# Down stages: activation sums on VectorE among the gate/up pairs, first output chunks through ScalarE and adding transfers

## The chip, the cores and the metric

One core of one Trainium2 chip runs the whole kernel as one launch. The time is the device time of that launch in microseconds (us). Below, PE is TensorE, DVE is VectorE, ACT is ScalarE, POOL is GpSimd and SP is SyncE; SP issues most plain transfers, and POOL issues all adding ones (transfers that add what they bring to what stands in the tile).

## The reference, cut to what matters

Two layers act on h, 512 tokens of width 1024, all in float32. The hidden width of a SwiGLU is 2816.

```python
h += 0.5 * swiglu(rmsnorm(h), w_gate, w_up, w_down)      # FFN1
h += W_out @ mixer(rmsnorm(h))     # layer 0: banded + dilated attention; layer 1: 2-D neighbourhood attention
h += 0.5 * swiglu(rmsnorm(h), w_gate, w_up, w_down)      # FFN2
h += sigmoid(rmsnorm(h) @ W_gate) * (p[i] @ W_ple)       # gate with a per-layer input

def swiglu(x, w_gate, w_up, w_down):
    return (jax.nn.silu(x @ w_gate) * (x @ w_up)) @ w_down
```

The change touches the four products with `w_down` (2816 x 1024), what stands just ahead of them (the gate and up products), and the norm that follows each.

## The kernel before, in words

**Precision.** Every float32 product is three matmuls of a reduced type: an operand x is split into hi, a copy made by ACT (L148), and lo = x - hi, made mostly by DVE (L149); then hi·hi + lo·hi + hi·lo is summed in PSUM.

**Gate and up.** The hidden width is cut into 22 chunks of 128, and `ffn` (L401 on) makes each by one "pair" (gate and up together). Pairs 0 to 3 (`pair_front`) use the chunks `xg` of h that are not yet divided by the root mean square, and multiply by it afterwards; pair 4 (`pair`) and pairs 5 to 21 (`pair_fast`, seven half-size products in place of eight, L371 to L373) use chunks split again by `halves` between the first pairs. A pair leaves one activation tile a[m], 128 x 512.

**Down.** `down` (L435 on) computes the product with w_down by seven half-size products in place of eight. The 2816 rows are halved into a[0..10] and a[11..21] (K2 = 11 chunks each), the 512 tokens into a left and a right 256, the 1024 columns into two halves. Four weight quarters b11, b12, b21, b22 are brought in six units of up to two chunks. A unit's product is 12 matmuls of 128 x 512 (L463 to L465), one whole product 66. The seven products run in three phases:

- phase 1, per unit: r1 from x1 (a[k] after its right half lost that of a[11+k], L432) and b11; r2 from x2 (a[11+k]) and b21; r3 from x1 and b11+b12;
- phase 2: rb from x3 and b12+b22; r1 goes on with b11 added, rc with b21 added too. x3 and the left half of a[11+k] are sums of activations, made in place by POOL (L510, L511, L513);
- phase 3: r3 goes on with b22 and x4 (the left half of a[11+k]).

Weights of a unit come by SP into one of five `wr` tiles (`load`), the sums of quarters are made in place by adding transfers that POOL issues (`add`, L454), and `parts` splits the tile anew after each. So POOL's queue holds both the sums of activations and the adding transfers, in the order in which a scheduler placed them at build time.

**The tail of a down stage.** After phase 3 the results stand with tokens on the partitions. For each of the eight chunks m of h, PE transposes four blocks into one of two `tr` banks (L545), and DVE adds half of them to the residual (L549), which SP had loaded from DRAM into `hs` (L538). `norm_split` then makes the next norm's hi (ACT, L211) and lo (DVE, L212), `norm_square` the square (ACT, L217) and its sum over chunks (L224, on POOL for most). POOL stores the chunk back (L562, L580). Chunks 0 to 3 take their halves from r1/r2 and rc, chunks 4 to 7 from c22 (ready after phase 2) and c2 (ready after phase 3). After FFN1 the mixer's projections read these splits; after FFN2 `ple` does: its first gate matmuls (L173 to L175) run chunk by chunk as the splits come.

## Time and profile before

| what | value |
|---|---|
| time, median of 3 (lowest, highest) | 2138.43 us (2136.97, 2143.73) |
| the profiled execution: its own time, its span | 2138.97 us, 2137.2 us |
| PE busy | 2032.2 us (95%) |
| DVE busy | 1620.7 us (76%) |
| ACT busy | 1131.5 us (53%) |
| POOL busy | 526.1 us (25%) |
| mean granted PE clock | 0.981 |

A row of a group reads: line, engine, operation, tile written <- tiles read, shapes, count | busy us, mean ns of one | idle time of the engine ahead of them, and what ended it. A row of windows reads: from:to in us, length, then busy us (and count) of PE, PEld, DVE, ACT and POOL, the granted PE clock, the share of time for which the 16 DMA engines were busy, and GB/s. A row of the chain of waits reads: start, length, who. A row of transfers reads: tile <- source, queue, count, KB each, median us from issue to landing. The four down stages are the windows that begin at 238.7, 900.3, 1327.7 and 1922.9 us.

### The profile page before, as it was taken

How to read it: one execution, taken by the hardware profiler on the slowest of the kernel's cores; microseconds unless marked ns; L12 is line 12 of the kernel's file. 1: busy time of each engine (PE TensorE's matmuls, PEld its weight loads, DVE VectorE, ACT ScalarE, POOL GpSimd, SP SyncE). 2: the span in 40 equal slices, each digit the busy share in tenths (PEclk: the TensorE clock that was granted, in tenths of full speed). 3: DMA queues.
4: the chain of work that ended last, by engine and by line, in shares of the span. 5: the costliest groups of instructions: out<-in, count | busy, mean ns of one | idle time of the engine just before them, and what ended most of it. 6: DMA issues, size and time to landing. Idle time of an engine off the chain costs nothing.

```text
span 2137.2 us, 33010 instructions
## 1 busy us (share of the span) xinstructions
PE 2032.2 (95%) x12294; PEld 1785.7 (84%) x12294; DVE 1620.7 (76%) x2571; ACT 1131.5 (53%) x1902; POOL 526.1 (25%) x534
## 2 busy tenths in 40 slices
PE   9999979899999999979899999798999999998888
PEld 6999857779788899957688999577888889996766
DVE  8787966688766887876678878767788587888575
ACT  5455645477645455645454556454666445554542
POOL 0011642432212001371320013713000200128231
PEclk9999989999999999999999999999999999999899
DMA  6677589543325576579554775796433446656971
GB/s 199 169 190 184 135 189 264 136 89 90 94 60 172 131 186 183 149 176 195 206 161 125 189 185 149 175 192 209 124 109 95 158 123 183 178 147 164 193 251 40
DMA packets 128049, 339.10 MB, mean 159 GB/s; under 512 B 23824, under 2 KB 31504, under 8 KB 127888
## 3 DMA queue, kind: packets, MB, share of 16 engines
q1 hardware_dynamic: 97728, 241.52, 34.3%
q0 software_dynamic: 30016, 95.44, 25.4%
q8 instruction: 96, 1.57, 0.3%
q14 instruction: 65, 0.53, 0.1%
q10 hardware_dynamic: 144, 0.04, 0.0%
HBM read 308.62 MB, written 17.27 MB: 152 GB/s over the span
## 4 chain that ended last, share of the span: by engine, by line
PE 69%; DVE 10%; DMA 7%; issue 6%; POOL 4%; ACT 3%; SPq 0%; DVEq 0%; POOLq 0%; ACTq 0%
PE mm L373 6%; PE mm L372 6%; PE mm L371 6%; PE mm L174 6%; PE mm L173 6%; PE mm L175 6%; DMA wr<-in_dn_dram 5%; DVE wl L149 3%; PE sc L373 3%; PE sc L372 3%; PE sc L371 3%; PE sc L173 2%; PE sc L175 2%; PE sc L174 2%; DVE act L212 1%
## 5 line engine op out<-in xcount | busy, mean ns | idle before, releaser
L148 ACT ACTIVATE wh<-wr 128x1024 fp32r<-128x1024 f32 (+1 forms) x503 | 516.0, 1029 | 577.7 <-DMA wr<-in_dn_dram 148.5
L149 DVE TENSOR_TENSOR wl<-wr,wh 128x1024 fp32r<-128x1024 f32 (+1 forms) x503 | 632.7, 1262 | 223.0 <-ACT wh L148 219.8
L373 PE MATMUL mm<-act,wl 128*128 128x256 f32 x1088 | 307.9, 283 | 0.0
L372 PE MATMUL mm<-act,wh 128*128 128x256 f32 x1088 | 307.9, 283 | 0.0
L371 PE MATMUL mm<-act,wh 128*128 128x256 f32 x1088 | 307.9, 283 | 0.0
L174 PE MATMUL mm<-act,wh 128*128 128x512 f32 (+1 forms) x648 | 258.2, 399 | 4.4 <-DVE act L212 4.2
L173 PE MATMUL mm<-act,wh 128*128 128x512 f32 (+1 forms) x648 | 256.7, 398 | 3.9 <-DVE act L689 2.5
L175 PE MATMUL mm<-act,wl 128*128 128x512 f32 (+1 forms) x648 | 256.7, 396 | 3.3 <-DVE wl L149 3.3
L371 PEld LDWEIGHTS mm<-act,wh 128*128 128x128 f32 x1088 | 208.9, 192 | 0.2
L372 PEld LDWEIGHTS mm<-act,wh 128*128 128x128 f32 x1088 | 208.9, 192 | 0.2
L373 PEld LDWEIGHTS mm<-act,wl 128*128 128x128 f32 x1088 | 208.9, 192 | 0.0
L349 POOL DMA_DIRECT2D wr<-in_gu_dram x68 | 60.0, 882 | 495.7 <-DVE wl L149 195.0
L371 PE MATMUL sc<-act,wh 128*128 128x256 f32 x544 | 154.0, 283 | 0.0
L372 PE MATMUL sc<-act,wh 128*128 128x256 f32 x544 | 154.0, 283 | 0.0
L373 PE MATMUL sc<-act,wl 128*128 128x256 f32 x544 | 154.0, 283 | 0.0
L149 DVE TENSOR_TENSOR act<-act,act 128x512 fp32r<-128x512 f32 (+1 forms) x192 | 150.7, 817 | 4.2 <-ACT act L148 4.1
L174 PEld LDWEIGHTS mm<-act,wh 128*128 128x128 f32 x648 | 123.9, 191 | 31.8 <-DVE act L212 9.0
L224 POOL TENSOR_TENSOR ssq<-ssq,tmp 128x512 f32<-128x512 f32 x48 | 70.1, 1460 | 324.0 <-ACT tmp L217 323.3
L173 PEld LDWEIGHTS mm<-act,wh 128*128 128x128 f32 x648 | 123.4, 191 | 28.2 <-issue 2.7
L175 PEld LDWEIGHTS mm<-act,wl 128*128 128x128 f32 x648 | 123.8, 191 | 26.6 <-DVE wl L149 4.5
L454 POOL DMA_DIRECT2D wr<-in_dn_dram x96 | 83.8, 901 | 185.1 <-DVE wl L149 122.2
L464 PE MATMUL mm<-wl,act 128*128 128x512 f32 x264 | 104.7, 397 | 14.0 <-DVE wl L149 14.0
(232 smaller groups left out, 4883.2 us busy)
## 6 DMA issues: line engine op xcount, KB each, us to landing
wr<-in_gu_dram SPq DMA_DIRECT2D x176, 512.0 KB, 4.6
wr<-in_dn_dram SPq DMA_DIRECT2D x80, 512.0 KB, 4.5
wr<-in_dn_dram POOLq DMA_DIRECT2D x80, 512.0 KB, 6.9
wr<-in_gu_dram POOLq DMA_DIRECT2D x68, 512.0 KB, 5.5
rb<-in_gu_dram SPq DMA_DIRECT2D x68, 256.0 KB, 2.6
act<-kept SPq DMA_DIRECT2D x56, 256.0 KB, 5.1
wr<-in_qk_ab_dram SPq DMA_DIRECT2D x20, 512.0 KB, 4.1
kept<-act POOLq DMA_DIRECT2D x32, 256.0 KB, 2.4
```

Source lines behind the costliest of these rows:

```text
L148: self.put(self.nc.scalar.activation(hi, src, AF.Copy))
L149: self.put((lo_eng or self.nc.vector).tensor_tensor(lo, src, hi.bitcast(F32), op=ALU.subtract))
L173: mm(out, stat[0], mov[0], start=start, stop=False)
L174: mm(out, stat[0], mov[1], start=False, stop=False)
L175: return mm(out, stat[1], mov[0], start=False, stop=stop)
L224: self.last_sum = eng.tensor_tensor(self.acc, self.acc, sq, op=ALU.add)
L349: nc.gpsimd.dma_start(rs, w[:, :UNIT], accum_op=ALU.add)
L371: mm(out, w[0][:, c], xs[k][0][:, x], start=start and k == 0, stop=False, skip_group_check=True)
L372: mm(out, w[0][:, c], xs[k][1][:, x], start=False, stop=False, skip_group_check=True)
L373: mm(out, w[1][:, c], xs[k][0][:, x], start=False, stop=stop and k == half - 1, skip_group_check=True)
L454: nc.gpsimd.dma_start(raw, b[:, u.start * T:u.stop * T], accum_op=ALU.add)
L464: mm(p, xh, wl, start=False, stop=False, skip_group_check=True)
```

## The change

- The halves that the down product combines are now the even and the odd hidden chunks: A = a[0::2], B = a[1::2]. The host lays out w_down to match.
- POOL does no arithmetic for the down product. `inner_sums` makes the three 256-wide operations of a chunk pair on DVE, for 9 of the 11 pairs right after the odd gate/up pair that completes it, for the other two in `down`; x3's source is a tile of its own (`sums`). The left half of B is updated on DVE.
- Pair 4 is made by `pair_front`, and `pair` is gone. `halves` splits only the left half of a first-half chunk.
- c2's copy and u3 stand ahead of the last rc product.
- Chunks 0 to 3 of h are transposed among the units of phase 3: ACT evicts each with a factor of 0.5 (L543 in the new numbering), and an adding transfer issued by POOL adds the residual from DRAM (L544). SP loads only the residuals of chunks 4 to 7. The transposes of c22 stand behind phase 3's units 4 and 5. All stores of h stand at the end (L572).
- After down stages the squares are summed on DVE. The first v projection of a mixer takes one bank from the other PSUM pool.

```diff
@@ -31,8 +31,9 @@
 WARM = 12
-FRONT = 4
-FAST = range(5, NF)
+FRONT = 5
+READY = 9
+SPLIT = 2
@@ -220,7 +221,7 @@
         else:
-            eng = nc.vector if c == KC - 1 or self.k == 0 else nc.gpsimd
+            eng = nc.vector if c == KC - 1 or self.k in (0, 1, 3, 5, 7) else nc.gpsimd
@@ -301,20 +302,6 @@
             self.mm3(p, (u[0][:, c:c + P], u[1][:, c:c + P]), xs[k], k == 0, k == KC - 1)
-    def pair(self, w, y):
-
...
-        nc.scalar.activation(t, pgu[0], AF.Silu)
-        nc.vector.tensor_tensor(t, pgu[1], t, op=ALU.mult)
-        return t
-
@@ -323,7 +310,12 @@
             nc.vector.scalar_tensor_tensor(x, self.h[k], self.gain[:, self.k, k:k + 1], self.R, op0=ALU.mult, op1=ALU.mult)
-            out.append(self.split_chunk(x, nc.vector))
+            if k < KC // 2:
+                both = self.act(F32R)
+                out.append((both[:, :H], both[:, H:]))
+                self.split(x[:, :H], *out[-1])
+            else:
+                out.append(self.split_chunk(x, nc.vector))
@@ -407,32 +399,31 @@
         kept = io["xT"].rearrange("p c t -> c p t") if first else self.put_away()
-        x1 = [None] * K2
+        x1, sums = [None] * K2, [None] * K2
...
             if m == NF - 1:
-                for k in range(2):
-                    self.lead_part(x1, a, k)
-            if m < FRONT:
-                r = self.pair_front(gu[i, m], m, first, gu[i, m + 1])
-            elif m in FAST:
-                r = self.pair_fast(gu[i, m], y, t)
-            else:
-                r = self.pair(gu[i, m], y)
+                for k in range(SPLIT):
+                    x1[k] = self.split_chunk(a[2 * k], nc.vector)
+            r = self.pair_front(gu[i, m], m, first, gu[i, m + 1]) if m < FRONT else self.pair_fast(gu[i, m], y, t)
             a.append(r)
+            if m % 2 and m // 2 < READY:
+                sums[m // 2] = self.inner_sums(*a[m - 1:])
...
         self.begin_norm(k_next)
-        self.down(dn[i], a, x1, kept)
-
-    def lead_part(self, x1, a, k):
-
-        if x1[k] is None:
-            right = slice(T // 2, T)
-            self.nc.gpsimd.tensor_tensor(a[k][:, right], a[k][:, right], a[K2 + k][:, right], op=ALU.subtract)
-            x1[k] = self.split_chunk(a[k], self.nc.vector)
-
-    def down(self, w, a, x1, kept):
+        self.down(dn[i], a, x1, sums, kept)
+
+    def inner_sums(self, a, b):
+
+        l, r = slice(0, T // 2), slice(T // 2, T)
+        s, tt = self.act(), self.nc.vector.tensor_tensor
+        tt(a[:, r], a[:, r], b[:, r], op=ALU.subtract)
+        tt(s[:, r], a[:, r], a[:, l], op=ALU.subtract)
+        tt(s[:, l], s[:, r], b[:, r], op=ALU.add)
+        return s
+
+    def down(self, w, a, x1, sums, kept):
@@ -440,7 +431,7 @@
         copy, tt, sub = nc.scalar.activation, nc.vector.tensor_tensor, ALU.subtract
-        pool = nc.gpsimd.tensor_tensor
+        A, B = a[0::2], a[1::2]
@@ -480,12 +471,15 @@
                 for k in ks(u):
-                    self.lead_part(x1, a, k)
+                    if sums[k] is None:
+                        sums[k] = self.inner_sums(A[k], B[k])
+                    if x1[k] is None:
+                        x1[k] = self.split_chunk(A[k], nc.vector)
...
                 for k in ks(u):
-                    x2[k] = self.split_chunk(a[K2 + k], nc.vector)
+                    x2[k] = self.split_chunk(B[k], nc.vector)
@@ -507,76 +501,74 @@
             if s < n:
...
                 for k in ks(u):
-                    pool(a[k][:, r], a[k][:, r], a[k][:, l], op=sub)
-                    pool(a[k][:, l], a[k][:, r], a[K2 + k][:, r], op=ALU.add)
-                    x3[k] = self.split_chunk(a[k], nc.vector)
-                    pool(a[K2 + k][:, l], a[K2 + k][:, l], a[k][:, r], op=ALU.add)
+                    x3[k] = self.split_chunk(sums[k], nc.vector)
+                    tt(B[k][:, l], B[k][:, l], sums[k][:, r], op=ALU.add)
                 product(rb, u, self.parts(raws[s]), x3, l, True, True)
...
                 add(raws[s - 1], b21, u)
+            if s == n + 1:
+                c2 = copied(r1)
+                u3 = [self.act(), self.act()]
+                for i in range(2):
+                    tt(u3[i], c2[i], rb[i], op=sub)
             if s > 1:
...
                     x4[k] = t[:, l], t[:, r]
-                    self.split(a[K2 + k][:, l], *x4[k])
-        c2, c21 = copied(r1), [self.act(), self.act()]
-        u3 = [self.act(), self.act()]
+                    self.split(B[k][:, l], *x4[k])
+        c21 = [self.act(), self.act()]
         for i in range(2):
-            tt(u3[i], c2[i], rb[i], op=sub)
             tt(c21[i], rc[i], u3[i], op=ALU.add)
+        for i in range(2):
             tt(c5[i], c5[i], u3[i], op=sub)
-        c22 = c5
-
-        hs = []
-        for m in range(KC):
-            hs.append(self.act())
+        c22, M = c5, KC // 2
+
+        hs = [self.act() for _ in range(KC)]
+        for m in range(M, KC):
             nc.sync.dma_start(hs[m], kept[m])
-        for u in units:
-            raw = load(b22, u)
-            product(r3, u, self.parts(raw), x4, l, False, True)
         def turned(out, x, j):
...
                 nc.tensor.transpose(out[:, i * P:(i + 1) * P], y[:, j * P:(j + 1) * P], self.ident)
-        def done(m, p, c):
-            h = hs[m]
-            nc.vector.scalar_tensor_tensor(h[:, c], p, 0.5, h[:, c], op0=ALU.mult, op1=ALU.add)
-            self.h[m] = h
-            if c.stop == T and c.start == 0:
-                self.norm_split(m)
-            else:
-                self.norm_split(m, c)
-
-        M = KC // 2
-        for m in range(M):
-            p = self.tbank()
+        def first_half(m):
+            p, h = self.tbank(), hs[m]
             turned(p[:, l], c11, m)
             turned(p[:, r], c21, m)
-            done(m, p, slice(0, T))
-            nc.gpsimd.dma_start(self.kept[m], hs[m])
-            self.norm_square(m)
-        for m in range(0, M, 2):
+            nc.scalar.activation(h, p, AF.Copy, scale=0.5)
+            nc.gpsimd.dma_start(h, kept[m], accum_op=ALU.add)
+            self.h[m] = h
+            self.norm_split(m)
+
+        def second_half(m, x, c):
             p = self.tbank()
             for j in range(2):
-                turned(p[:, j * H:(j + 1) * H], c22, m + j)
+                turned(p[:, j * H:(j + 1) * H], x, m - M + j)
             for j in range(2):
-                done(M + m + j, p[:, j * H:(j + 1) * H], r)
+                h = hs[m + j]
+                nc.vector.scalar_tensor_tensor(h[:, c], p[:, j * H:(j + 1) * H], 0.5, h[:, c], op0=ALU.mult, op1=ALU.add)
+                self.h[m + j] = h
+                self.norm_split(m + j, c)
+
+        for i, u in enumerate(units):
+            raw = load(b22, u)
+            product(r3, u, self.parts(raw), x4, l, False, True)
+            if i in (2, 3):
+                first_half(2 * i - 4)
+                first_half(2 * i - 3)
+            elif i > 3:
+                second_half(M + 2 * i - 8, c22, r)
         for c in (l, r):
...
                 tt(c2[i][:, c], r3[i][:, c], c2[i][:, c], op=sub)
-        for m in range(0, M, 2):
-            p = self.tbank()
-            for j in range(2):
-                turned(p[:, j * H:(j + 1) * H], c2, m + j)
-            for j in range(2):
-                done(M + m + j, p[:, j * H:(j + 1) * H], l)
-        for m in range(M, KC):
+        for m in range(M, KC, 2):
+            second_half(m, c2, l)
+        for m in range(KC):
             nc.gpsimd.dma_start(self.kept[m], hs[m])
@@ -655,11 +647,11 @@
         return out
-    def project_v(self, src, view, rcol, parts=True):
-
-
-        nc = self.nc
-        banks = [self.bank(), self.bank()]
+    def project_v(self, src, view, rcol, parts=True, banks=None):
+
+
+        nc = self.nc
+        banks = banks or [self.bank(), self.bank()]
@@ -852,7 +844,8 @@
             if i < 2:
-                f = lambda: v.__setitem__(key, self.project_v(io["v_ab"][i], nat, self.rcol))
+                f = lambda: v.__setitem__(key, self.project_v(io["v_ab"][i], nat, self.rcol, banks=None if i else [
+                    self.sbank(), self.bank()]))
@@ -1169,7 +1162,7 @@
                 fill.append((("v", n // 2), 2, lambda i=n // 2: vs.__setitem__(
-                    i, self.project_v(io["v_c"][i], nat, self.rcol))))
+                    i, self.project_v(io["v_c"][i], nat, self.rcol, banks=None if i else [self.sbank(), self.bank()]))))
@@ -1375,7 +1368,7 @@
 def _quarters(w):
-    return w.reshape(2, K2, P, 2, T).transpose(0, 3, 2, 1, 4).reshape(4, P, K2 * T)
+    return w.reshape(K2, 2, P, 2, T).transpose(1, 3, 2, 0, 4).reshape(4, P, K2 * T)
```

POOL's queue at the first down stage (`act` are activation tiles, `wr` weight tiles; lines 432 to 513 are the sums, 454 the adding transfers). Before:

```order
L510 TENSOR_TENSOR act_283<-act_283 128x256
L511 TENSOR_TENSOR act_283<-act_283,act_1417 128x256
L510 TENSOR_TENSOR act_365<-act_365 128x256
L511 TENSOR_TENSOR act_365<-act_365,act_1541 128x256
L432 TENSOR_TENSOR act_1169<-act_1169,act_2533 128x256
L454 DMA wr_2774<-in_dn_dram 128x1024
L513 TENSOR_TENSOR act_1417<-act_1417,act_283 128x256
```

and now (445 is the line of the adding transfers of weights):

```order
L341 DMA wr_2677<-in_gu_dram 128x1024
L445 DMA wr_2807<-in_dn_dram 128x1024
L445 DMA wr_2852<-in_dn_dram 128x1024
L445 DMA wr_2921<-in_dn_dram 128x1024
L445 DMA wr_2990<-in_dn_dram 128x1024
```

The sums are gone from between the transfers, whose own order is what it was.

ACT's queue at the end of the first down stage (`wh_3937` and the like are the first splits of the mixer's weights, L211 is hi, L217 the square). Before:

```order
L148 ACTIVATE wh_3872<-wr_3871 128x1024
L148 ACTIVATE wh_3937<-wr_3936 128x1024
L148 ACTIVATE wh_3991<-wr_3990 128x1024
L211 ACTIVATE act_3725<-act_3601,gain 128x512
L217 ACTIVATE ssq_3730<-act_3601 128x512
L211 ACTIVATE act_3738<-act_3603,gain 128x512
L217 ACTIVATE tmp_3743<-act_3603 128x512
```

and now (L543 is the eviction, L212 hi, L218 the square):

```order
L543 ACTIVATE act_3611<-tr_3677 128x512
L149 ACTIVATE wh_3882<-wr_3881 128x1024
L212 ACTIVATE act_3684<-act_3611,gain 128x512
L218 ACTIVATE ssq_3826<-act_3611 128x512
L543 ACTIVATE act_3612<-tr_3688 128x512
L149 ACTIVATE wh_3947<-wr_3946 128x1024
L149 ACTIVATE wh_4001<-wr_4000 128x1024
L212 ACTIVATE act_3695<-act_3612,gain 128x512
L218 ACTIVATE tmp_3829<-act_3612 128x512
L543 ACTIVATE act_3613<-tr_3717 128x512
L212 ACTIVATE act_3724<-act_3613,gain 128x512
```

The eviction of a chunk now stands behind hi and square of the chunk before it. On POOL the adding transfer of a chunk and its store stand in turn:

```order
L544 DMA act_3611<-in_xT_dram 128x512
L572 DMA kept_2800<-act_3611 128x512
L544 DMA act_3612<-in_xT_dram 128x512
L572 DMA kept_2800<-act_3612 128x512
L544 DMA act_3613<-in_xT_dram 128x512
```

A store reads the tile that the adding transfer ahead of it writes.

7 lines of the change are left out of this document (removed).

## The prediction, made before the changed kernel ran

> **What bounds the kernel now.** First the page: busy shares and the granted clock.
>
> ```profile
> PE 2032.2 (95%) x12294; PEld 1785.7 (84%) x12294; DVE 1620.7 (76%) x2571; ACT 1131.5 (53%) x1902; POOL 526.1 (25%) x534
> PEclk9999989999999999999999999999999999999899
> ```
>
> PE is busy 95% of the span, so what can be won is idle PE and matmuls at a lower clock, together about 100 us. The windows over the four down stages, and one dense stretch of the same matmuls, show where that lies. Columns: window, length, busy us (count) of PE, PEld, DVE, ACT, POOL, granted clock, DMA share, GB/s.
>
> ```profile
> 238.70:364.70 126.00, 113.26 (x465) 89.27 (x464) 89.11 (x96) 62.17 (x89) 56.17 (x52) 0.95 0.84 203
> 900.30:1027.20 126.90, 111.37 (x464) 88.41 (x463) 89.43 (x96) 62.03 (x89) 56.16 (x52) 0.96 0.83 203
> 1327.70:1454.10 126.40, 113.18 (x464) 89.25 (x463) 88.12 (x94) 61.27 (x89) 56.16 (x52) 0.95 0.83 198
> 1922.90:2050.80 127.90, 113.27 (x464) 89.80 (x463) 89.61 (x96) 62.18 (x89) 56.21 (x52) 0.93 0.83 201
> 984.00:1008.00 24.00, 24.00 (x108) 19.87 (x107) 12.16 (x18) 10.60 (x16) 4.33 (x5) 1.00 0.92 190
> ```
>
> A dense matmul takes about 0.2265 us (24.00 us hold 106 of them, the two at the edges counted as parts). A stage has 7 x 66 = 462: 104.6 us dense. The four take 126.0 + 126.9 + 126.4 + 127.9 = 507.2, so 507.2 - 418.5 = 88.7 us are lost there, 22.2 in each: nearly all that the run loses. The first stage cut by phase (phase 1 ends at 297.6, phase 2 at 349.7):
>
> ```profile
> 238.70:272.00 33.30, 30.67 (x132) 24.08 (x131) 33.30 (x30) 20.98 (x30) 31.26 (x27) 1.00 0.64 155
> 272.00:297.60 25.60, 17.94 (x69) 12.97 (x67) 15.06 (x14) 7.39 (x12) 13.63 (x13) 0.92 0.82 186
> 297.60:309.00 11.40, 8.95 (x22) 6.32 (x23) 5.45 (x7) 5.54 (x8) 3.46 (x4) 0.65 1.03 216
> 309.00:349.70 40.70, 40.70 (x177) 33.56 (x177) 26.31 (x37) 22.31 (x34) 7.82 (x9) 0.98 0.91 197
> 349.70:364.70 15.00, 15.00 (x68) 12.35 (x67) 9.00 (x12) 5.95 (x6) 0.00 (x0) 1.00 0.95 344
> ```
>
> Phases 1 and 2 are 198 matmuls each, 44.85 us dense. Phase 1 takes 58.9 (lost 14.0), phase 2 52.1 (lost 7.3), phase 3 nothing. In the first window DVE is busy all the time and POOL nearly so, with the DMA at 0.64; then the DMA saturates (1.03) and the clock falls to 0.65. The chain of waits through that place:
>
> ```profile
> 283.69 7.64 DMA wr<-in_dn_dram
> 291.90 0.86 POOL wr L454
> 296.63 7.04 DMA wr<-in_dn_dram
> 303.76 1.06 ACT wh L148
> ```
>
> So the stage is late twice: DVE paces phase 1, which delays adding transfers that POOL issues behind its sums, and these then pile up and set the start of phase 2.
>
> **The change part by part. POOL's sums go.** Splits on DVE, in 246 to 272 (POOL adding, two rows) and in 311 to 345 (POOL mostly idle, two rows), then POOL's sums in the whole run:
>
> ```profile
> L149 DVE TENSOR_TENSOR act<-act,act 128x512 fp32r<-128x512 f32 x14 | 16.1, 1184 | 0.0
> L149 DVE TENSOR_TENSOR wl<-wr,wh 128x1024 fp32r<-128x1024 f32 x8 | 13.5, 1688 | 0.0
> L149 DVE TENSOR_TENSOR wl<-wr,wh 128x1024 fp32r<-128x1024 f32 x10 | 12.2, 1223 | 11.0 <-ACT wh L148 11.0
> L149 DVE TENSOR_TENSOR act<-act,act 128x512 fp32r<-128x512 f32 x5 | 3.4, 685 | 0.0
> L432 POOL TENSOR_TENSOR act<-act,act 128x256 f32<-128x256 f32 x44 | 34.1, 775 | 233.9 <-DVE act L398 233.9
> L513 POOL TENSOR_TENSOR act<-act,act 128x256 f32<-128x256 f32 x44 | 60.7, 1389 | 5.6 <-ACT act L148 2.9 <-DVE act L149 2.8
> ```
>
> The same DVE splits take 1184 and 1688 ns while POOL adds, 685 and 1223 without it. With the lower durations, 14 x 0.50 + 8 x 0.465 = 10.7 of DVE's 26 us in that window go: DVE no longer paces phase 1, and the adding transfers issue as soon as their tile is split. What takes DVE's place is the DMA. Its busy time in phases 1 and 2 is share by length: 33.3 x 0.64 + 25.6 x 0.82 + 11.4 x 1.03 + 40.7 x 0.91 = 91.1 us, against 89.7 of dense matmuls. The bytes stay, so even a full DMA leaves 91.1 + 15.0 (phase 3) = 106.1 per stage. At phase 3's share, 0.95, it is 95.9 + 15.0 = 110.9; at 0.91, the share of the flowing part of phase 2, 100.1 + 15.0 = 115.1. I take 0.95, since with DVE free the five `wr` tiles turn round without that pause: 4 x 110.9 = 443.6, a gain of **63.6 us**; bounds 507.2 - 460.4 = 47 and 507.2 - 424.4 = 83.
>
> **The sums among the gate/up pairs.** Front pairs, other pairs, a 256-wide DVE sum, and DVE's wait in each pair:
>
> ```profile
> 30.00:62.00 32.00, 32.00 (x142) 26.20 (x141) 31.85 (x55) 15.96 (x25) 1.96 (x2) 1.00 0.56 112
> 80.00:200.00 120.00, 120.00 (x1002) 120.00 (x1002) 96.51 (x132) 63.89 (x95) 14.89 (x18) 1.00 0.70 181
> L335 DVE TENSOR_TENSOR tmp<-tmp,tmp 128x256 f32<-128x256 f32 x16 | 6.7, 420 | 0.0
> L381 DVE TENSOR_TENSOR act<-mm,act 128x256 f32<-128x256 f32 x68 | 28.9, 424 | 55.2 <-ACT act L380 55.2
> ```
>
> Three sums of 0.42 are 1.26 us per two pairs. In the pairs DVE is busy 96.5 of 120 and stands still 55.2 / 68 = 0.81 us at L381 in each, under a PE that is never idle: hidden. In the front pairs DVE is full (31.85 of 32), and the change gives it a few sums more there; in return pair 4 no longer waits for `halves`. I cost the whole at nothing. Without the cover it is 9 x 1.26 = 11.3 us per FFN at most, 45 in all; that PE is at 32.00 of 32.00 with DVE full already says that the cover holds.
>
> **The tail.** Chunks 0 to 3 leave DVE and SP for ACT and an adding transfer. The rows: eviction, hi, square, sum of squares on POOL and DVE, hi of a half chunk, adding and plain transfers of POOL, and the two kinds of tail from the end of phase 3's third unit on (mixer behind, `ple` behind).
>
> ```profile
> L470 ACT ACTIVATE act<-mm 128x512 f32<-128x512 f32 x16 | 8.5, 584 | 0.0
> L211 ACT ACTIVATE act<-act,gain 128x512 fp32r<-128x512 f32 x48 | 34.0, 716 | 20.9 <-DVE act L1317 10.4 <-DVE act L744 7.8 <-DMA act<-in_xT_dram 2.0
> L217 ACT ACTIVATE tmp<-act 128x512 f32<-128x512 f32 x62 | 37.7, 617 | 10.1 <-DVE act L1300 10.1
> L211 ACT ACTIVATE act<-act,gain 128x256 fp32r<-128x256 f32 x32 | 16.2, 506 | 15.4 <-DVE act L549 15.4
> L224 POOL TENSOR_TENSOR ssq<-ssq,tmp 128x512 f32<-128x512 f32 x48 | 70.1, 1460 | 324.0 <-ACT tmp L217 323.3
> wr<-in_dn_dram POOLq DMA_DIRECT2D x16, 256.0 KB, 5.2
> kept<-act POOLq DMA_DIRECT2D x32, 256.0 KB, 2.4
> 357.90:400.80 42.90, 36.27 (x219) 30.16 (x217) 29.30 (x42) 20.81 (x32) 15.28 (x16) 1.00 0.62 222
> 1020.40:1058.10 37.70, 29.87 (x135) 22.62 (x134) 28.17 (x36) 18.03 (x28) 17.62 (x17) 0.95 0.58 213
> ```
>
> In ACT's new order the eviction of a chunk stands behind hi of the one before, and that hi waits for the adding transfer. So the four chunks go one after another: 0.58 + 5.2 + 0.72 + 0.62 + 0.1 (handing over) = 7.2 us each. A new adding transfer of 256 KB to an h tile has no row; the nearest is the 5.2 of `wr`, below it stands POOL's plain store with 2.4, above it the 7.64 of the chain. Let Z be the end of phase 3's third unit. Eviction 0 ends at Z + 1.7 (four transposes and 0.58), hi 0 at 7.6, hi 3 at 7.6 + 3 x 7.2 = 29.2, its square at 29.8; then four times (2 x 0.506 + 0.617) = 6.5 for chunks 4 to 7: Z + 36.4. Queued behind the waiting ACT are the next weights' splits; on POOL each store waits for the adding transfer ahead of it, and behind it nothing urgent stands but the next chunk's transfer, which is late anyway; SP has four loads of 256 KB fewer, which the adding transfers bring instead; on PE the transposes of chunks 2 and 3 and of c22 wait for the two `tr` banks, so phase 3's last units do too. In `ple`'s tail the eighth chunk's matmuls start at about Z + 37.7 and two more pieces of 2.7 us follow: 43.1 against 37.7, 5.4 slower. In the mixer's tail, PE has other matmuls to fill with: 43.4 against 42.9. PE then idles in pieces of 4 to 5 us. Before, the pause near 290 was followed by 11.4 us at a clock of 0.65, which is 4.0 us of matmul time; I take 2 per tail (bounds 0 and 4). Together 2 x 7.4 + 2 x 2.5 = **20 us lost**, 12 to 28 with the bounds of the clock alone.
>
> The Trainium skill (TensorE: Matmul & The Clock Gate, What's actually happening) halves the clock after about 3.4 us of idle PE; the 0.65 behind a pause of some 4 us agrees, and by it the new pauses of 4 to 5 us would each cost a slow window, which is the upper bound above.
>
> **Small parts.** Sums of squares go from 1460 ns on POOL to DVE, where they lie behind the squares on ACT in either case; c2 ahead of the last product and the bank for v lie beside dense PE: nothing.
>
> **Sum.** 2139.0 - 63.6 + 19.8 = 2095.2 against the profiled execution; the median of the runs shown is 0.5 lower: **2095 us**. Its own range, bounds taken together: 2139 - 83 + 12 = 2068 to 2139 - 47 + 28 = 2120.
>
> **The rivals.**
>
> *The adding transfers land like stores (14 in 100).* If they take 2.4 us, a step is 4.4, hi 3 comes at Z + 4.8 + 13.2 = 18.0, and the tails gain instead of lose: ACT ends at 25.2, `ple`'s tail 6.4 sooner than before, the mixer's by about 3 (its matmuls, less the wait for POOL's sums): 19 in all, so 2139 - 64 - 19 = 2056. For it: 256 KB is small and the DMA is at 0.58 to 0.62 there. Against: 5.2 is a median of 16 adding transfers. By the Trainium skill (DMA: Bandwidth & Descriptors, Anatomy of one DMA — SWDGE path) such a transfer would be about 2.0 + 262144/436000 = 2.6 us, an estimate, and so near this rival; the rows of adding transfers here, 5.2, do not agree.
>
> *Phase 2 keeps its late start (18 in 100).* If the adding transfers still take 7 us and still set the start of phase 2 and the slow clock after it, only what DVE costs goes. PE idles 33.30 - 30.67 + 25.60 - 17.94 = 10.3 us in phase 1, about 4 of it in the pause behind the transfer: 6.3 x 4 = 25 gained, 20 lost: 2134. For it: 1.03 at 216 GB/s. Against: the DMA at 0.64 earlier, which leaves 12 us of room to pull them into.
>
> *The tail eats the gain (8 in 100): slower.* The next weights load while the adding transfers run (344 GB/s in phase 3; 512 KB loads of that time are on the chain):
>
> ```profile
> 354.02 7.96 DMA wr<-in_qk_ab_dram
> ```
>
> Sixteen adding transfers stand in series. Each us above 5.2 costs 16 us in all, so from 5.2 + (63.6 - 19.8) / 16 = 7.9 us on the change is slower than before. At 8.5 the tails lose 20 + 53 = 73: 2148. Against it: 7.64 and 7.04 are for 512 KB in a saturated queue.
>
> **How the numbers follow.** The forecast has 55 in 100, the rivals 14, 18 and 8; 5 are left for mixtures near no change. The range 2060 to 2135 holds the forecast's own and the second rival, and leaves out most of the first and all of the third. Less than 0.3%, 6.4 us, can't be told from no change. Faster by more: 55 + 14 + most of 18 and a part of the rest, 0.84; the same 0.06; slower 0.10.
>
> **What would show it.** Right: down stages of about 111 us, DVE's splits near 690 and 1223 ns in phase 1, the DMA share there above 0.9, no pause of 4 us ahead of phase 2; in the tails, ACT's hi of chunks 0 to 3 each ended by an adding transfer of some 5 us and 7 us apart, and `ple`'s tail near 43 us with a lower clock. Wrong: stages still above 118 us (DMA sets phase 2), tails shorter than 37 us (transfers quick), or hi more than 8 us apart; PE idle among the gate/up pairs would mean that DVE's new sums are not hidden.

## The result, and the profile after

The changed kernel took 2119.56 us (median of 4; 2114.56 to 2122.82) against 2141.08 us of the kernel before, run beside it (median of 4): ratio 0.9899, 95% interval 0.987 to 0.9927. It is faster, by 21.5 us or 1.0%. The forecast was a gain of 43 us: the time lies inside the range that was given, the gain is half of the forecast. Its profiled execution has a span of 2112.8 us, 24.4 less than before. The page of the changed kernel:

```profile
PE 2014.7 (95%) x12294; PEld 1786.2 (85%) x12294; DVE 1593.2 (75%) x2763; ACT 1134.0 (54%) x1918; POOL 305.5 (14%) x350
```

POOL has lost 221 us of work, DVE has gained 192 instructions and yet is busy 28 us less. Where the time went is read from the starts of the matmuls of each stretch in the two traces (us; the last column is the sum over the row):

| stretch | before | after | after - before |
|---|---|---|---|
| start to the first fast gate/up pair | 67.3 | 70.6 | +3.3 |
| fast pairs, each FFN | 171.4 | 171.4 | 0 |
| phase 1 | 59.0, 59.9, 59.6, 60.2 | 48.0, 48.6, 47.7, 47.3 | -47.1 |
| phase 2 | 52.1, 52.1, 51.8, 52.7 | 52.8, 52.5, 52.8, 55.2 | +4.6 |
| start of phase 3 to the next fast pairs, or to the last matmul | 379.2, 144.1, 312.4, 93.9 | 382.8, 147.6, 316.2, 98.1 | +15.1 |

In the last row the first and third numbers hold a mixer, the second and fourth the layer gate. The rows add up to -24.1, the spans differ by 24.4; the rest is rounding. Phase 1 gives 11.8 us per stage, phase 2 loses 1.2, and some of the gain is given back in the tails. Windows of the changed kernel over its first down stage: phase 1, the start of phase 2, the rest of it, phase 3 with its transposes, the seam of phases 1 and 2, and last the slow part of that seam (columns as before):

```profile
241.90:289.90 48.00, 45.11 (x200) 37.02 (x199) 37.62 (x56) 28.57 (x42) 8.50 (x10) 1.00 0.85 203
289.90:300.00 10.10, 4.04 (x15) 3.02 (x16) 2.84 (x4) 3.12 (x5) 2.00 (x4) 0.76 1.07 212
300.00:342.70 42.70, 42.70 (x186) 35.27 (x185) 26.86 (x38) 23.58 (x38) 9.49 (x11) 0.98 0.89 182
342.70:366.30 23.60, 18.54 (x83) 14.79 (x82) 11.97 (x16) 8.78 (x11) 2.29 (x3) 0.94 0.83 260
272.00:300.00 28.00, 19.05 (x82) 15.11 (x81) 10.52 (x14) 10.59 (x16) 7.04 (x9) 0.91 0.97 218
295.10:301.90 6.80, 2.92 (x7) 2.37 (x8) 3.46 (x4) 4.55 (x7) 1.07 (x2) 0.50 1.07 197
```

Phase 1 is nearly dense. The loss of phase 2 lies in its first 12 us: PE is busy only 4.04 of the first 10.1 with the DMA at 1.07, and the granted clock is 0.50 from 295.1 to 301.9. After that PE is dense. DVE in 246 to 272 (groups by form):

```profile
L150 DVE TENSOR_TENSOR wl<-wr,wh 128x1024 fp32r<-128x1024 f32 x10 | 12.2, 1216 | 0.1
L150 DVE TENSOR_TENSOR act<-act,act 128x512 fp32r<-128x512 f32 x16 | 10.6, 680 | 0.0
```

The splits take 680 and 1216 ns here, against 1184 and 1688 while POOL added. The tail on ACT, from its timeline (start, length, instruction; in brackets the idle time ahead and what ended it):

```profile
353.18 0.58 ACT L543 ACTIVATE act<-tr 128x512 f32<-128x512 f32 x1
...
361.17 0.72 ACT L212 ACTIVATE act<-act,gain 128x512 fp32r<-128x512 f32 x1 [4.28 <-DMA act<-in_xT_dram]
...
362.32 0.58 ACT L543 ACTIVATE act<-tr 128x512 f32<-128x512 f32 x1
...
368.82 0.58 ACT L543 ACTIVATE act<-tr 128x512 f32<-128x512 f32 x1
375.88 0.72 ACT L212 ACTIVATE act<-act,gain 128x512 fp32r<-128x512 f32 x1 [6.49 <-DMA act<-in_xT_dram]
...
377.03 0.58 ACT L543 ACTIVATE act<-tr 128x512 f32<-128x512 f32 x1
382.61 0.72 ACT L212 ACTIVATE act<-act,gain 128x512 fp32r<-128x512 f32 x1 [5.00 <-DMA act<-in_xT_dram]
```

The four evictions (L543) stand 9.1, 6.5 and 8.2 us apart. Three of the four hi (L212) are ended by the adding transfer of their chunk; the second (367.68, not shown) stands behind other work on ACT. The transfers themselves (tile, queue, count, KB, median us to landing), and what PE waited for longest in 342 to 420 (total, times, longest): the transposes for the evictions, and the first projections of the mixer (L174) for hi.

```profile
act<-kept POOLq DMA_DIRECT2D x12, 256.0 KB, 4.6
act<-in_xT_dram POOLq DMA_DIRECT2D x4, 256.0 KB, 5.4
```

```profile
PE ob L174 <- ACT act L212: 4.2, 2, 3.6
PE tr L537 <- ACT act L543: 4.2, 1, 4.2
```

### The profile page after: what moved, and what is told of

It reads as the page before. It is cut to its first block, busy times and chain, and to the rows that moved or that the text cites. A ratio compares the mean times of both kernels' runs of the same rounds, so it can differ in the third digit from the quotient of the medians.

```text
span 2112.8 us, 32943 instructions
## 1 busy us (share of the span) xinstructions
PE 2014.7 (95%) x12294; PEld 1786.2 (85%) x12294; DVE 1593.2 (75%) x2763; ACT 1134.0 (54%) x1918; POOL 305.5 (14%) x350
## 4 chain that ended last, share of the span: by engine, by line
PE 79%; DMA 8%; issue 5%; ACT 3%; DVE 3%; POOL 1%; SPq 0%; POOLq 0%; DVEq 0%; ACTq 0%
PE mm L365 6%; PE mm L363 6%; PE mm L364 6%; PE mm L175 6%; PE mm L174 6%; PE mm L176 6%; DMA wr<-in_dn_dram 5%; PE sc L364 3%; PE sc L365 3%; PE sc L363 3%; PE sc L176 2%; PE sc L174 2%; PE sc L175 2%; PE mm L454 2%; PE mm L455 2%
## 5 line engine op out<-in xcount | busy, mean ns | idle before, releaser
L150 DVE TENSOR_TENSOR wl<-wr,wh 128x1024 fp32r<-128x1024 f32 (+1 forms) x503 | 597.0, 1191 | 201.7 <-ACT wh L149 199.2
L174 PE MATMUL mm<-act,wh 128*128 128x512 f32 (+1 forms) x648 | 256.5, 398 | 8.7 <-ACT act L212 7.6
L174 PEld LDWEIGHTS mm<-act,wh 128*128 128x128 f32 x648 | 123.6, 191 | 33.9 <-ACT act L212 10.2
L150 DVE TENSOR_TENSOR act<-act,act 128x512 fp32r<-128x512 f32 (+1 forms) x192 | 114.8, 622 | 3.6 <-ACT act L149 3.5
L149 ACT ACTIVATE act<-act 128x512 fp32r<-128x512 f32 (+1 forms) x192 | 103.0, 568 | 4.1 <-DVE act L1244 2.1
L365 PEld LDWEIGHTS sc<-act,wl 128*128 128x128 f32 x544 | 104.5, 192 | 0.0
```

The costliest lines, as they stand in the source:

```text
L149: self.put(self.nc.scalar.activation(hi, src, AF.Copy))
L150: self.put((lo_eng or self.nc.vector).tensor_tensor(lo, src, hi.bitcast(F32), op=ALU.subtract))
L174: mm(out, stat[0], mov[0], start=start, stop=False)
L365: mm(out, w[1][:, c], xs[k][0][:, x], start=False, stop=stop and k == half - 1, skip_group_check=True)
```

## The experiments

Ratios are against the kernel before, run on the same chip; "together" means phases 1 and 2 of a stage. The stretches come from matmul starts in each trace, as in the table above.

### The tail: order on ACT, or the adding transfers

First the order alone. hi of the four chunks is made after all evictions have been issued:

```diff
-            self.norm_split(m)            # in first_half
...
                 first_half(2 * i - 3)
+                if i == 3:
+                    for m in range(M):
+                        self.norm_split(m)
```

> The changed kernel, with hi and square of chunks 0 to 3 made only after all four evictions have been issued, so that no eviction waits on ACT behind an adding transfer. If the order on ACT is what stretches the tail (my theory), the pauses of 4.3 and 5.1 us of PE before the transposes of the fourth chunk, and the slow clock after them, go away: 5 to 8 us per stage, 2119.6 - 20 to 32 = 2088 to 2100. If instead the adding transfers themselves are what the next norm waits for (rival), the pause only moves to the first matmuls of the mixer or of the layer gate: less than 2 us per stage, 2112 to 2120.

Measured: 2116.12 us, ratio 0.9898 (0.9883 to 0.9913): the same as the change. Phase 3, 21.3 to 24.3 us in the changed kernel, shrank to between 17.0 and 17.5, so that pause was ACT's order; but what follows it grew. The four stretches from phase 3 on change by -5.3, +2.6, +1.8 and +1.6 us. In the second stage, PE then waited 4.7 us ahead of c2's transposes, and the clock was low (waits in 996 to 1050; window):

```profile
PE tr L537 <- DVE act L570: 5.1, 2, 4.7
```

```profile
1010.00:1060.00 50.00, 38.91 (x145) 28.46 (x146) 31.41 (x55) 24.64 (x39) 15.61 (x14) 0.86 0.47 154
```

That is the rival's outcome, but for the first stage. Then the whole old tail in the changed kernel (SP loads eight residuals, transposes after phase 3, `done` on DVE):

```diff
-        for m in range(M, KC):
+        for m in range(KC):
             nc.sync.dma_start(hs[m], kept[m])
...
-            nc.scalar.activation(h, p, AF.Copy, scale=0.5)
-            nc.gpsimd.dma_start(h, kept[m], accum_op=ALU.add)
+            nc.vector.scalar_tensor_tensor(h[:, c], p, 0.5, h[:, c], op0=ALU.mult, op1=ALU.add)
...
-            if i in (2, 3):               # and all transposes behind phase 3
```

> The changed kernel with the tail of the kernel before: eight residual loads by SP, all transposes after phase 3, additions on DVE. From the third phase's start to the next stage the changed kernel took 3.5 to 4.1 us longer than the one before in each of four stages, so if that is the price of the new tail alone (theory), the time falls by 15: 2105. If the loss comes from elsewhere, as from the sums on DVE or from what the shorter phase 1 leaves to be loaded later (rival), the old tail is no quicker here: 2117 to 2123.

Measured: 2085.11 us, ratio 0.9746 (0.9729 to 0.9763). By the ratios the new tail costs 33 us, twice what the comparison with the kernel before had shown. The four stretches from phase 3 on are 369.8, 144.3, 306.4 and 93.1 us: 13.0, 3.3, 9.8 and 5.0 less than with the new tail. So in the stretches with a mixer some other part of the change had gained 9.4 and 6.0 us on the kernel before, and the new tail had hidden it.

Which half of the new tail costs? The transposes stay among phase 3's units, but DVE adds the residual:

```diff
-            nc.scalar.activation(h, p, AF.Copy, scale=0.5)
-            nc.gpsimd.dma_start(h, kept[m], accum_op=ALU.add)
+            nc.vector.scalar_tensor_tensor(h, p, 0.5, h, op0=ALU.mult, op1=ALU.add)
```

> The changed kernel with the transposes of chunks 0 to 3 left among the units of phase 3, but the residuals loaded by SP and added by DVE, no eviction by ACT and no adding transfer in the tail. With the whole old tail the time was 2085. If ACT's waits for the adding transfers are what the new tail costs (theory), this kernel is as quick or up to 12 us quicker: 2073 to 2087. If moving the transposes among the matmuls is itself the cost, through the two banks or DVE (rival), it stays at 2105 or above.

Measured: 2082.28 us, ratio 0.9736 (0.9722 to 0.9751). So the place of the transposes costs nothing over the whole kernel, and ACT's evictions with their adding transfers are the cost: 35 us by the ratios. The stretches are 371.0, 139.1, 311.0 and 90.3: shorter than the old tail ahead of the layer gate, longer ahead of a mixer. That was then used:

```diff
+        among = self.k in (3, 7)          # the layer gate follows
...
-            if i in (2, 3):
+            if among and i in (2, 3):
...
+        if not among:                     # first_half and c22 behind phase 3
```

> The changed kernel with DVE adding the residuals, the transposes of chunks 0 to 3 and c22 among phase 3's units only where the layer gate follows, and behind phase 3 where a mixer follows. The profiles of the two pure forms had the layer gate's stretches at 139.1 and 90.3 against 144.3 and 93.1 us, the mixers' at 371.0 and 311.0 against 369.8 and 306.4. If those differences are of the tails alone (theory), both gains add up: 2085 - 8 = 2077, 2074 to 2079. If they are noise of one execution (rival), 2081 to 2085.

Measured: 2076.11 us, ratio 0.9702 (0.9685 to 0.9718), with 368.2, 140.4, 306.1 and 90.4. Both gains add.

### What had shortened the mixers

Two edits that I had costed at nothing, each undone in the kernel with the old tail:

```diff
-    self.project_v(..., banks=None if i else [self.sbank(), self.bank()])
+    self.project_v(..., banks=None)
```

> The changed kernel with the old tail and the first v projection in its old bank. With the old tail the stretches from phase 3 to the next gate/up pairs were 9.4 and 6.0 us shorter than before where a mixer lies in them, and not shorter where the layer gate does. If the bank is the reason (theory), those 15 us come back: 2098 to 2102. If the sums of squares on DVE are (rival), 2083 to 2088.

```diff
-            eng = nc.vector if c == KC - 1 or self.k in (0, 1, 3, 5, 7) else nc.gpsimd
+            eng = nc.vector if c == KC - 1 or self.k == 0 else nc.gpsimd
```

> The changed kernel with the old tail and the squares summed on GpSimd as before. If the bank of the v projection made the mixers shorter (theory), this costs at most 4 us: 2083 to 2089. If the squares on DVE did (rival), the 15 us come back: 2098 to 2102.

Measured: 2089.33 us, ratio 0.9772 (0.9758 to 0.9787) with the old bank; 2096.76 us, 0.9803 (0.9787 to 0.982) with the squares on POOL. Each lies just outside the nearer forecast (2083 to 2088 and 2098 to 2102). The theory of the bank falls for the most part: by the ratios the squares on DVE carry some 12 us, the bank some 5. By stretches, the squares on POOL make the mixers 376.3 and 311.8 in place of 369.8 and 306.4, the old bank 374.0 and 306.0. So the bank counts in the first mixer alone, where PE waits 2.5 us for the evictions at L685. Its profile is also 5.0 us longer from the start to the first fast pair, which the bank does not touch, so its share by the ratio is uncertain.

How the squares act is read from the kernel with the old tail and DVE, and the one with POOL. First the sums of squares (groups of 341 to 400):

```profile
L225 DVE TENSOR_TENSOR ssq<-ssq,tmp 128x512 f32<-128x512 f32 x7 | 4.8, 683 | 0.0
```

```profile
L225 POOL TENSOR_TENSOR ssq<-ssq,tmp 128x512 f32<-128x512 f32 x6 | 8.5, 1423 | 0.2
```

then the lo of the half chunks, which DVE makes beside them (the same groups, in the same order):

```profile
L213 DVE SCALAR_TENSOR_TENSOR act<-act,gain,act 128x256 fp32r<-128x256 f32 x8 | 3.8, 479 | 0.0
```

```profile
L213 DVE SCALAR_TENSOR_TENSOR act<-act,gain,act 128x256 fp32r<-128x256 f32 x8 | 6.6, 833 | 0.0
```

then a wait of PE with POOL (345 to 385), which the kernel with DVE does not have:

```profile
PE ob L175 <- DVE act L213: 3.6, 4, 1.9
```

and the first 35 us from the start of phase 3 (old tail with DVE, old tail with POOL, and the changed kernel):

```profile
341.30:376.30 35.00, 34.52 (x185) 28.93 (x184) 29.76 (x50) 19.50 (x30) 4.39 (x8) 1.00 0.82 292
```

```profile
341.00:376.00 35.00, 30.29 (x141) 22.91 (x140) 29.37 (x41) 17.87 (x28) 12.79 (x14) 0.99 0.79 278
```

```profile
342.70:377.70 35.00, 26.36 (x127) 21.44 (x126) 18.41 (x28) 13.18 (x18) 4.29 (x6) 0.94 0.80 247
```

While POOL adds the squares, DVE's lo takes 833 ns in place of 479, the mixer's first projections wait for it, and PE stands still 4.2 us longer in these 35. That is most of the 6.5 us of the first mixer; in the second it is 3.3 of 5.4. The root mean square comes later too: POOL's instruction for it (L235) starts 35.6, 39.5 and 49.4 us after phase 3 has begun. But PE's pauses lie ahead of that, and in the first mixer PE has no wait for it; in the second it waits 1.1, 1.1 and 1.7 us (L251).

### Phase 2: bytes, tiles, chain or seam

The sixth unit's weights go into the two rb tiles, which frees wr tiles:

```diff
+            if u.stop - u.start == 1:
+                raw = self.tp.tile([P, T], F32, tag="rb", name=self.nm("rb"), bufs=2)
```

> The changed kernel, with the sixth unit's weights (one chunk, 128x512) in the two rb tiles, which the down stage leaves idle, so that the five wr tiles serve the other units and the first loads of phase 2 can start sooner. If phase 2 starts late because its first sums of weights get their tiles late (theory), the pauses of 3.1 and 6.2 us at its start shrink: 4 to 7 us per stage, 2119.6 - 16 to 28 = 2092 to 2104. If the adding transfers around the start only share one saturated DMA (rival), they collide with the last ones of phase 1 and less than 1.5 us per stage is won: 2114 to 2120.

Measured: 2117.77 us, ratio 0.99 (0.9883 to 0.9917): no gain. The pause behind rb fell from about 6 to 3 us, but phase 1 grew from 48 to 50.3 to 50.8. Next, the last of the four transfers per unit is left out, so that rc's sum lacks b21:

```diff
-                add(raws[s - 1], b21, u)
```

> The changed kernel without the adding transfer of b21 in phase 2, one of four transfers per unit; the sum that rc uses lacks b21. Phase 2 takes 52.8 us in the first stage, of which 44.85 are dense matmuls. If its own DMA work (48.8 us of busy DMA) bounds it (theory 1), it falls to 45 to 47 us, and the kernel by about 4 x 6 = 24 us. If the pauses at its start come from the time that the first sums take from load to adding transfer (theory 2), the b21 transfers come too late to matter and phase 2 stays at 50 to 53 us.

Measured in a single execution: phase 2 took 54.4, 52.2, 53.0 and 53.0 us. The windows of its phase 1, the start of phase 2 and the rest:

```profile
240.50:289.30 48.80, 45.16 (x201) 36.94 (x199) 37.62 (x56) 28.57 (x42) 8.75 (x11) 1.00 0.84 200
289.30:303.00 13.70, 8.43 (x21) 6.25 (x22) 5.63 (x7) 4.91 (x7) 2.57 (x3) 0.66 0.87 172
303.00:343.70 40.70, 40.70 (x179) 33.59 (x179) 26.29 (x38) 22.93 (x35) 3.49 (x4) 0.99 0.61 135
```

In the rest the DMA share falls from 0.89 to 0.61 and no time is won, since PE was dense there already. Theory 1 (phase 2's own bytes) falls; the loss is at the seam of the two phases. The first two sums placed earlier, with the rb tiles and the old tail:

```diff
         for s in range(n + 1):
+            if s >= n - 1:
+                early[s - n + 1] = summed(s - n + 1)
```

> The changed kernel with the old tail, the sixth unit's weights in the two idle rb tiles, and the first two sums of weights of phase 2 (load and adding transfer) placed ahead of phase 1's last two units. Leaving the b21 transfers out left phase 2 at 52 to 54 us, so its length is set at its start. If those sums only come late (theory), the pauses of 2.6 and 6.8 us and the slow clock behind them shrink by 4 to 6 us per stage: 2085 - 16 to 24 = 2061 to 2069. If the adding transfers of the two phases' seam are limited by what the DMA moves (rival), phase 1 grows by what phase 2 loses: 2080 to 2090.

Measured: 2084.82 us, ratio 0.9752 (0.9738 to 0.9767), the same as the old tail alone (0.9746). Phase 2 was 49.5 to 53.1, phase 1 49.6 to 51.8: together 102.3 in the mean against 101.8. What one phase wins the other gives. Fewer adding transfers instead: b22 by plain loads and a sum on DVE:

```diff
-            add(raws[s], b22, units[s])
+            for k in ks(units[s]):
+                side = self.tp.tile([P, T], F32, tag="rb", name=self.nm("rb"), bufs=2)
+                nc.sync.dma_start(side, b22[:, k * T:(k + 1) * T])
+                c = slice((k - units[s].start) * T, (k - units[s].start + 1) * T)
+                tt(raws[s][:, c], raws[s][:, c], side, op=ALU.add)
```

> The changed kernel with the old tail, and in phase 2 b22 is brought by plain loads of 256 KB by SP into the idle rb tiles and added to b12 on DVE, instead of by an adding transfer: one of three adding transfers per unit less. Phases 1 and 2 together took 101 to 103 us in every kernel so far, whether the sums were placed earlier or the last transfer left out. If the adding transfers at the seam of the phases, at some 200 GB/s against some 360 of plain loads, are what bounds it (theory), two units' sums come 1 to 2.5 us sooner each: 2 to 5 us per stage, 2085 - 8 to 20 = 2065 to 2077. If only the number of bytes counts, or DVE has no room at the seam (rival), 2083 to 2092.

Measured: 2074.24 us, ratio 0.9698 (0.9677 to 0.9719), about 10 us better than the old tail alone and within the theory's range. In its profiled execution, which was slower than its median (span 2078.2), phases 1 and 2 took 100.5 in the mean; in the two kernels at the end, which have this edit too, 99.1 and 99.3. Then the two that were to part the chain of the first sums (theory B) from a full DMA (theory A). PE's work into the seam:

```diff
-            if s:
+            if 0 < s < n - 1:
                 product(r3, u, self.parts(raws[s - 1]), x1, r, True, True)
...
+            if s < 2:                     # in phase 2, behind rb's units
+                product(r3, units[n - 2 + s], self.parts(left[s]), x1, r, True, True)
```

> The changed kernel with the old tail, where r3's fifth and sixth units of phase 1 are multiplied inside phase 2, behind rb's first and second unit. At the seam PE has only rb's first two units (5.4 us) to do until b11 has been added to the first sum, which takes 6 to 8 us after that sum was split. If this chain is what makes phase 2 52 to 55 us long (theory B), the 18 matmuls moved there fill up to 4 us of it: 2085 - 8 to 16 = 2069 to 2077. If the DMA is simply full at the seam (theory A), the same transfers take as long and the pauses only move: 2082 to 2088.

and traffic out of it, without adding b12 in r3's last two units:

```diff
-                add(raw, b12, u)
+                if s < n - 2:
+                    add(raw, b12, u)
```

> The changed kernel with the old tail, without adding b12 to the last two units in phase 1 (r3 of those units uses b11 alone): 0.75 MB of adding transfers less, just ahead of phase 2. If the DMA is full at the seam (theory A, some 200 GB/s), phases 1 and 2 together shorten by up to 3.8 us, from 102 to 98 us per stage: about 2070. If the chain of the first sums sets it (theory B), r3's last pause goes but phase 2 waits as before: 100 to 102 us together, 2078 to 2085.

Measured: 2079.91 us, ratio 0.9708 (0.9687 to 0.9729), and 2078.88 us, 0.9704 (0.9673 to 0.9736). The first time lies between the two forecasts, the second at the quick end of theory B's. By the ratios both are 8 to 9 us quicker than the old tail alone, but the kernel before took 2137 to 2146 us on that chip, and the spans are only 3.2 and 5.0 us shorter; so I go by the stretches. The eight kernels here whose phases 1 and 2 are those of the change have 101.2 to 102.3 us together, each in the mean of its stages. With the matmuls moved, phase 1 is 42.2 and phase 2 59.1: together 101.3, so nothing is won, against theory B. With the two transfers left out it is 99.9, below all eight: 1.9 us less per stage than with the old tail alone, half of what theory A gave at most and hardly below the 100 of theory B. The seam in windows, of the first and of the second:

```profile
270.00:302.00 32.00, 26.67 (x110) 19.85 (x108) 14.47 (x18) 12.46 (x18) 9.58 (x11) 1.00 0.97 212
```

```profile
272.00:300.00 28.00, 20.94 (x85) 16.57 (x84) 12.50 (x16) 12.98 (x19) 7.52 (x9) 0.92 0.97 210
```

and of the kernels with the old tail, without b21, and with b22 by plain loads:

```profile
270.00:300.00 30.00, 20.93 (x86) 16.66 (x85) 12.41 (x17) 12.16 (x18) 7.88 (x9) 0.90 0.97 216
```

```profile
272.00:300.00 28.00, 19.09 (x74) 14.79 (x73) 8.98 (x11) 9.82 (x15) 7.00 (x8) 0.89 0.96 208
```

```profile
272.00:302.00 30.00, 23.49 (x88) 17.49 (x87) 18.17 (x26) 13.06 (x19) 4.32 (x5) 0.84 0.79 205
```

In four of the five the DMA was full for some 30 us around the seam, at 208 to 216 GB/s, whatever PE did there. This fits theory A as far as the moves go that won nothing. But A isn't all, and the cause of the seam is not settled between the two: half of its price came in, and with b22 by plain loads the share fell to 0.79, yet phases 1 and 2 took 100.5 us; in the first stage PE's pauses became 1.2, 2.0, 1.3 and 2.1 us in place of 2.4 and 6.7. The chain of waits of the changed kernel shows both at once:

```profile
278.62 1.24 DVE wl L150
279.87 7.91 DMA wr<-in_dn_dram
288.87 8.39 DMA wr<-in_dn_dram
```

DVE's split frees a tile, into which b12 is then loaded and b22 added, one behind the other, as in theory B; and in the full DMA these take 7.91 and 8.39 us, where the medians of the whole run are 4.7 and 7.2, as in theory A. What bounds the seam of the kernel with plain loads (the two rb tiles, which take turns, or DVE's queue) was not tried.

### The front, and the parts together

In the first FFN the sums of the first two pairs of chunks are made after pairs 5 and 7:

```diff
+            late = (5, 7) if first else ()
...
-            if m % 2 and m // 2 < READY:
+            if m % 2 and m // 2 < READY and not (late and m < 4):
```

> The changed kernel with the old tail, where in the very first FFN the sums of the first two pairs of chunks are made after pairs 5 and 7, not among the front pairs 1 and 3. The first fast pair began at 67.3 us before, at 68.9 to 70.6 in the changed kernels. If the sums on a full DVE are why (theory), it begins at 67.5 or sooner, and the time is 2081 to 2084; if the pair that moved to the front form is (rival), it stays at 69 to 71 and the time at 2085.

Measured: 2081.56 us, ratio 0.9732 (0.9718 to 0.9747), which alone can't be told from the 0.9746 of the old tail; but the first fast pair began at 66.4 us, against 68.9 there. Waits in 40 to 60 and a window of the changed kernel:

```profile
PE mm L176 <- DVE wl L150: 2.0, 1, 2.0
```

```profile
46.00:53.00 7.00, 5.02 (x16) 3.64 (x15) 7.00 (x10) 1.85 (x4) 0.00 (x0) 0.76 0.40 119
```

DVE was full, a split of weights came 2 us late, and PE stood; with the sums moved the wait is gone. The three kernels with this edit begin the fast pairs at 66.4 to 66.6 us, the others with the change at 68.7 to 73.9. Together, the tail by kind, b22 by DVE and this:

> Old addition of residuals on DVE, the tail by kind, b22 by plain loads and DVE, the very first sums after the front: the three that were quicker than the old tail alone by 11, 9 and 4 us. If they are of different stretches, as the profiles say, they add: 2085 - 24 = 2061, 2056 to 2068. If the 11 of b22 was in part noise of its batch (its profile showed phases 1 and 2 only 5 us shorter in all), 2066 to 2072.

Measured: 2066.48 us, ratio 0.9652 (0.962 to 0.9684). The changed kernel has 0.9899: the difference is 53 us of the time before. By the ratios it is 20 us quicker than the old tail alone, where the three parts sum to 24: they nearly add up, and the time lies where the two forecasts overlap. It beats both kernels. With r3's units in the seam as well:

> The one before with r3's last two units inside phase 2 as well. With theory B 8 to 16 us quicker than it: 2045 to 2055. With theory A the same as it within 3 us.

Measured: 2066.25 us, ratio 0.965 (0.9624 to 0.9675): the same, against theory B's 8 to 16 us, in a second setting.

## Why the prediction was right or wrong

| term | forecast | measured |
|---|---|---|
| phases 1 and 2 | -63.6 | -42.5 |
| sums among the pairs and the front | 0 | +3.3 |
| tails | +19.8 | +31.1 |
| small parts | 0 | -16.0 |
| sum | -43.8 | -24.1 |

Measured are the profiled executions; tails and small parts are parted by the kernel with the old tail (13.0 + 3.3 + 9.8 + 5.0, and -9.4 + 0.2 - 6.0 - 0.8 in the four stretches).

**DVE in phase 1: right.** The splits fell to 680 and 1216 ns, where 685 and 1223 were forecast, and phase 1 to 47.9 us in the mean, 3 above dense.

**Phases 1 and 2 at a DMA share of 0.95: wrong, and the step that failed.** I added the DMA's busy time of both phases (91.1 us) and spread it at 0.95, giving 95.9; they took 101.2. In the first stage the share over both is 0.89 (48.0 x 0.85 + 10.1 x 1.07 + 42.7 x 0.89 = 89.6 of 100.8 us), below even the 0.91 of the cautious bound. The forecast treats the transfers as if any could move into any free time. They can't: phase 1 ran at 0.85 with free time that the transfers of phase 2 did not use, and after the seam the DMA had room again (0.89) while PE was dense. Phase 2 stayed at 52 to 55 because of its start: in the first stage PE pauses 2.9 and 6.1 us, and from within the second pause on the clock is 0.50 for 6.8 us. A heap of transfers stands there in a full DMA; whether their bytes or their chain sets its length stays open. Nothing that only moved work across the seam shortened the two phases together, and taking adding transfers away there did a little. In this part the second rival described what happened; its price for phase 1 (6.3 us per stage) was too low, 11.8 were won.

**Gate/up pairs: right but for the front.** The fast pairs take 171.4 us in every kernel. The front pairs, which I had noted as full (31.85 of 32), were not cover: the start was 3.3 us longer than before in the changed kernel. The kernel that took the sums out of there shows it, with a start 0.9 shorter than before. The wait for DVE is 2.0 us, and the slow clock behind it costs some 1.7 (70.6 against 68.9 in the kernel with the old tail, which has the same wait at the full clock).

**Tails: right in the chain on ACT, wrong in the cover.** Steps of 9.1, 6.5 and 8.2 us against 7.2, and adding transfers of 4.6 and 5.4 us against 5.2. Ahead of the layer gate the cost was 3.3 and 5.0 where 7.4 stood. Ahead of a mixer it was 13.0 and 9.8 where 2.5 stood: I let other matmuls fill the time. But what PE came to next were the transposes and the first projections, and these wait for the evictions and for hi. In the first 35 us PE is busy 26.36 us in place of 34.52 with the old tail, and over the whole first stretch its work takes 369.2 us in place of 365.3, in part at the lower clock: together 12.1 of the 13.0.

**Small parts at nothing: wrong.** I had priced POOL's adding as a brake on DVE in phase 1, and left it out in the tail. There the sums of squares on POOL make DVE's lo slower, and the first projections wait for it: 12 us in the two mixers by the ratios. The bank gave 4.2 us, in the first mixer alone.

**The quick adding transfers** did not come. By the Trainium skill (DMA: Bandwidth & Descriptors, Anatomy of one DMA — SWDGE (gpsimd) path), 256 KB should land in an estimated 2.6 us; the adding transfers of the tails have 4.6 to 5.4, so the measurement decides against it for them. POOL's plain stores of that size had a median of 2.9 in the changed kernel. One figure of that rival was also off: with its own steps `ple`'s tail is 25.2 + 1.3 + 5.4 = 31.9 us against 37.7, a gain of 5.8 and not 6.4.

## What to carry to other kernels

Where a sum prices one engine as a brake on another in one stage, look for the same pair in the other stages: POOL's adding slowed DVE's splits in phase 1 and its lo in the tail, and only the first was in the sum. Matmuls cover a wait only if they stand ahead of it in PE's order and do not need the same chunks. An average DMA share says what could move, not what does; where a few buffers chain load, addition, split and product, look at the window around the seam. A net comparison hid a cost of 31 us behind a gain of 16 until one part was undone.

## What the hardware showed that I had not expected

Adding transfers were slow: 256 KB landed in a median of 4.6 to 5.4 us in the tails, and in the seams, where adding transfers and loads together filled the DMA (share 0.96 to 1.07), it moved 208 to 218 GB/s, against 344 at a share of 0.95 in phase 3 of the kernel before, where plain loads ran. A pause of PE of only 2.0 us can be followed by the low clock: in the window 46 to 53 of the changed kernel it is 0.76, while in the kernel with the old tail the same pause of 2.0 us was followed by dense matmuls at a clock of 1.00.
